# First FFN: eight up pairs as seven block products, and the weight sums of the last parts made by VectorE in the down products

## The chip, the core and the metric

The kernel runs on one core of a Trainium2 chip. A core has a matrix engine (TensorE, PE in the profile), a vector engine (VectorE, DVE), a scalar engine (ScalarE, ACT), GpSimd (POOL) and SyncE (SP); each works through its own list of instructions in order, and waits at an instruction until the semaphores that it names have come. The metric is the time of one execution in microseconds, the median of 3 runs.

## The reference

Two layers, each a mixer and then an FFN; the change lies in the FFN. With 528 positions (512 and 16 meta tokens), model width 1024 and FFN width 2816:

```python
def ffn_sublayer(h, pre_g, post_g, w_up, conv_w, w_down):
    u = rms_norm(h, pre_g)
    z = jnp.einsum("bld,df->blf", u, w_up)
    z = causal_depthwise_conv(z, conv_w)
    g, up = jnp.split(z, 2, axis=-1)
    y = jnp.einsum("blf,fd->bld", jax.nn.silu(g) * up, w_down)
    return h + rms_norm(y, post_g)
```

`w_up` is 1024 x 5632 and `w_down` 2816 x 1024 in each layer.

## The kernel before

**Matrix products.** All is float32. A matrix is split into a high and a low half that TensorE multiplies at full rate, and a product is three passes: high by high, high by low, low by high. `mm3` (L786) issues them for a list of blocks of 128 input channels. ScalarE makes the high half of a weight chunk by a cast (L601, `whi<-raw`), VectorE the low half by a subtraction (L602, `wlo<-raw,whi`). `prep_one` does this for one chunk of 512 KB: a load on SP's queue into one of three `raw` tiles, the cast, the subtraction. `next_w` calls it so that three chunks are ahead of the one that TensorE multiplies.

**The FFN of one layer.** The 2816 channels are 22 pairs: pair f has a gate chunk (f) and an up chunk (22 + f), of 128 channels each. They come in three parts, PARTS = (8, 7, 7). Within a part, each pair makes its two up products of 96 matmuls in all (8 blocks x 3 passes x 2 halves of 264 positions, twice), is copied from PSUM to `zs`, convolved (`gate_conv`: ACT L2120, then DVE L2122 twice), passed through silu (ACT L2132), multiplied (DVE L2133) and split into y (ACT L2136, DVE L2140). After a part, its down product runs in eight steps m, one for each 128 output channels; `yp` takes the result (ACT L2351 after part 0, DVE L2353 after part 1). The third part's down product is fused with the end of the layer.

**Seven block products.** For a pair listed in SEVEN, `seven_pair` takes the gate and up product together as a 2 x 2 block product (two halves of the input channels, two halves of the positions) and makes it with seven block products in place of eight: `product` (L2234) issues one, 4 blocks x 3 passes = 12 matmuls over half of the positions, so that a pair takes 84 matmuls in place of 96. It needs four weights: the first is half the plain gate and half plain; the three others (called c, b and d here, tags `whi`, `shi` and `y`) hold sums of blocks of the gate and up weights and come from a DRAM tile `w_sum`. It also needs sums of blocks of the input, `t0` to `t3`, which `normalised` builds while part 0 and its down product run. The results stand in PSUM and are combined by ScalarE's copies (L2260 to L2280).

Before, only layer 1 works so (SEVEN_IN), with 12 of its 22 pairs: 8 to 13 in part 1, 15 to 20 in part 2. The other tiles of a seven pair's weights are loaded into `h`: after part 0 of such a layer, h is written to DRAM, its space (four tiles of 512 KB, `spare`) serves as further raw tiles for four of every seven loads, and h is loaded back when the last seven pair is issued.

**The weight sums.** All 12 are made by DMA alone. `sum_steps` returns four steps: three copies into `w_sum` on SP's queue, and three accumulating DMAs on GpSimd's queue, one behind the other (L533). `tick` spreads them: a tiny copy on GpSimd (L2152) that reads what is just finished holds the queue until then. Eight pairs' sums are made in layer 0's FFN, four in layer 1's mixer.

**Split weights for the next mixer.** `store_one` takes six chunks of layer 1's `w_in`, splits them ahead of time (ACT L615, DVE L616) and stores both halves (`w_split`) on GpSimd's queue. It is called in layer 0's two down products, at the odd steps m.

**What sets the order.** In the FFN, a scheduler places each instruction by modelled times; what is written first goes first where times agree. Each engine's list is fixed when the program is built. A tile that is used again makes its next writer wait for its last reader.

## Time and profile before

| | |
|---|---|
| runs (3) | median 1282.54 us, 1281.57 to 1283.13 |
| the profiled execution | 1280.6 us, of which the span of the records is 1278.7 us |
| granted TensorE clock | 0.999 |
| layer 0's FFN | up part 0 from about 276 us, its down product from about 353 us, part 1 from about 400 us |
| layer 1's FFN | up part 0 to about 994 us, its down product to 1040.57 us |
| TensorE, up and down products of layer 0 | `mm3` L786 |
| seven block products (layer 1) | `product` L2234 |

The time includes about 2 us around the span. Busy time of an engine is the union of its instructions; the waits of TensorE, which has the least idle time, say where another engine or a transfer holds the kernel.

### The profile page before, as it was taken

The numbers are of one execution on the slowest core, as the hardware profiler recorded it, in microseconds if no ns is written. First come the engines' busy times: TensorE is split into PE (matmuls) and PEld (weight loads), VectorE is DVE, ScalarE is ACT, GpSimd is POOL, SyncE is SP. The second block draws the span as 40 slices with busy tenths as digits, with TensorE's granted clock in tenths as the row PEclk, the third lists the DMA queues.
The fourth block names the chain that finished last, engine by engine and source line by source line (L and its number), as shares of the span: only waits on it lengthen the run. The fifth ranks groups of instructions, "written<-read, shape, count | busy, mean of one in ns | idle before, by whom it ended". The sixth has DMA issues, their size and how long they took to land.

```text
span 1278.7 us, 24208 instructions
## 1 busy us (share of the span) xinstructions
PE 1259.6 (99%) x9660; PEld 1208.0 (94%) x9660; DVE 888.4 (69%) x1505; ACT 667.0 (52%) x1273; POOL 154.7 (12%) x333
## 2 busy tenths in 40 slices
PE   8999999999999999999999999999999999999997
PEld 8999899999999999999999998989999789979997
DVE  7888765688733774466587878765799738746964
ACT  7254577564333442233573546766554447626753
POOL 1313311001122112100003234120000000000000
PEclk9999999999999999999999999999999999999999
DMA  7136132705579647832461675536234235434611
GB/s 242 34 102 160 51 101 76 234 25 149 138 235 264 158 106 229 215 92 89 145 248 50 168 174 129 140 80 220 85 97 152 94 118 166 151 116 151 203 63 66
DMA packets 69393, 176.30 MB, mean 138 GB/s; under 512 B 7632, under 2 KB 18000, under 8 KB 69024
## 3 DMA queue, kind: packets, MB, share of 16 engines
q1 hardware_dynamic: 60784, 155.74, 38.4%
q0 software_dynamic: 8496, 19.01, 8.5%
q8 instruction: 76, 1.25, 0.4%
q14 instruction: 37, 0.30, 0.1%
HBM read 151.09 MB, written 37.95 MB: 148 GB/s over the span
## 4 chain that ended last, share of the span: by engine, by line
PE 93%; DVE 3%; ACT 1%; DMA 1%; issue 1%; POOL 0%; SPq 0%; DVEq 0%; ACTq 0%
PE psum L786 69%; PE psum L2234 9%; PE psum L1356 4%; PE psum L1620 3%; PE psum L1586 2%; PE psum L923 1%; PE psum L1542 1%; PE psum L1686 1%; PE psum L1272 1%; DMA raw<-in_w_dram 0%; DVE yp L999 0%; POOL dm L1557 0%; DMA h<-in_x_dram 0%; ACT whi L738 0%; DVE h L1009 0%
## 5 line engine op out<-in xcount | busy, mean ns | idle before, releaser
L786 PE MATMUL psum<-y,whi 128*128 128x264 f32 (+3 forms) x1968 | 384.1, 299 | 3.2 <-ACT yp L2351 1.7
L786 PE MATMUL psum<-uhi,whi 128*128 128x264 f32 (+1 forms) x1456 | 349.8, 288 | 2.7 <-DVE zs L2085 0.9
L786 PE MATMUL psum<-ulo,whi 128*128 128x264 f32 (+1 forms) x1456 | 343.4, 284 | 0.6 <-DVE ulo L2020 0.4
L786 PE MATMUL psum<-uhi,wlo 128*128 128x264 f32 (+1 forms) x1456 | 342.4, 284 | 0.0
L786 PEld LDWEIGHTS psum<-y,whi 128*128 128x128 f32 x1968 | 304.7, 188 | 17.5 <-ACT yp L2351 2.3
L786 PE MATMUL psum<-y,wlo 128*128 128x264 f32 (+3 forms) x984 | 272.7, 297 | 0.3 <-DVE wlo L742 0.3
L786 PEld LDWEIGHTS psum<-uhi,whi 128*128 128x128 f32 x1456 | 245.9, 188 | 7.4 <-issue 2.0
L786 PEld LDWEIGHTS psum<-ulo,whi 128*128 128x128 f32 x1456 | 246.0, 188 | 1.3 <-DVE ulo L2020 0.6
L786 PEld LDWEIGHTS psum<-uhi,wlo 128*128 128x128 f32 x1456 | 245.6, 188 | 0.0
L786 PEld LDWEIGHTS psum<-y,wlo 128*128 128x128 f32 x984 | 177.1, 188 | 5.7 <-DVE wlo L742 0.6
L601 ACT CAST whi<-raw 128x1024 fp32r<-128x1024 f32 (+1 forms) x80 | 82.2, 1029 | 114.4 <-PE psum L786 85.0
L2122 DVE SCALAR_TENSOR_TENSOR c<-zs,pv,c 128x528 f32<-128x528 f32 (+1 forms) x176 | 131.2, 757 | 11.2 <-ACT c L2120 9.2
L602 DVE TENSOR_TENSOR wlo<-raw,whi 128x1024 fp32r<-128x1024 f32 (+1 forms) x80 | 95.8, 1198 | 43.5 <-ACT whi L601 42.7
L742 DVE TENSOR_TENSOR wlo<-raw,whi 128x1024 fp32r<-128x1024 f32 (+2 forms) x80 | 95.6, 1204 | 29.8 <-ACT whi L738 29.3
L738 ACT CAST whi<-raw 128x1024 fp32r<-128x1024 f32 (+2 forms) x80 | 81.7, 1030 | 26.9 <-PE psum L786 20.0
L1102 DVE SCALAR_TENSOR_TENSOR cacc<-apad,pv,cacc 128x528 f32<-128x528 f32 x120 | 87.6, 772 | 0.1
L2120 ACT ACTIVATE c<-zs,pv 128x528 f32<-128x528 f32 (+1 forms) x88 | 63.2, 727 | 4.1 <-DVE zs L2272 1.5
L2136 ACT CAST y<-c 128x528 fp32r<-128x528 f32 (+1 forms) x44 | 27.6, 627 | 71.2 <-DVE c L2133 71.2
L2085 DVE TENSOR_TENSOR zs<-psum,rz 128x528 f32<-128x528 f32 x40 | 28.3, 707 | 47.7 <-PE psum L786 46.9
L1620 PE MATMUL psum<-pf,vals 128*128 128x400 f32 (+3 forms) x160 | 50.7, 399 | 0.6 <-POOL pf L1600 0.6
L1586 PE MATMUL psum<-q,k 128*128 128x128 f32 (+2 forms) x192 | 51.1, 348 | 0.0
L2132 ACT ACTIVATE c<-c 128x528 f32<-128x528 f32 (+1 forms) x44 | 28.1, 640 | 43.8 <-DVE c L2122 43.8
(265 smaller groups left out, 1972.5 us busy)
## 6 DMA issues: line engine op xcount, KB each, us to landing
raw<-in_w_dram SPq DMA_DIRECT2D x135, 512.0 KB, 4.3
raw<-in_w_dram SPq DMA_DIRECT2D x27, 448.0 KB, 4.4
h<-w_sum SPq DMA_DIRECT2D x14, 512.0 KB, 4.2
h<-in_w_dram SPq DMA_DIRECT2D x13, 512.0 KB, 3.8
w_sum<-in_w_dram SPq DMA_DIRECT2D x24, 256.0 KB, 8.5
w_sum<-in_w_dram SPq DMA_DIRECT2D x12, 512.0 KB, 7.3
w_sum<-in_w_dram POOLq DMA_DIRECT2D x12, 512.0 KB, 7.3
w_sum<-w_sum POOLq DMA_DIRECT2D x24, 256.0 KB, 5.6
```

Of the source, the lines that this page charges most:

```text
L601: nc.scalar.copy(hi[:, :sz], raw[:, :sz])
L602: nc.vector.tensor_sub(lo[:, :sz], raw[:, :sz], hi[:, :sz].bitcast(F32))
L738: nc.scalar.copy(box["hi"][:, :sz], box["raw"][:, :sz])
L742: nc.vector.tensor_sub(lo[:, :sz], box["raw"][:, :sz], box["hi"][:, :sz].bitcast(F32))
L786: nc.tensor.matmul(d, lhsT=w[a][:, k, cols], rhs=rhs(b, k, hf), start=start and i == 0 and p == 0, stop=stop and i == n - 1 and p == 2)
L1102: nc.vector.scalar_tensor_tensor(conv[j], in0=src, in1=conv[j], scalar=col("a_dw_w", CK * j + i), op0=ALU.mult, op1=ALU.add)
L1356: nc.tensor.matmul(ps[:n, :nw], lhsT=(uhi, ulo)[ui][:, k, P * b:P * b + n], rhs=w[wi][:, k % 4, :], start=k == 0 and p == 0, stop=k == KD ...
L1586: nc.tensor.matmul(s, lhsT=k[:, ka:ka + kn], rhs=q[:, s0:qz], start=i == 0, stop=i == 1)
L1620: nc.tensor.matmul(acc[:, s0 - qa:qz - qa], lhsT=vals[:, b].rearrange("p h d -> p (h d)")[:, o:o + P], rhs=box["p"], start=b == 0, stop=b ...
L2120: nc.scalar.activation(dst, src[:, 2:2 + 2 * fw], AF.Copy, scale=wtap(2, t))
L2122: nc.vector.scalar_tensor_tensor(dst, in0=src[:, i:i + 2 * fw], scalar=wtap(i, t), in1=dst, op0=ALU.mult, op1=ALU.add)
L2234: nc.tensor.matmul(psum[:, bank, :n7], lhsT=w[a][:, k0 + k, :], rhs=rhs(b, k), start=start and k == 0 and p == 0, stop=stop and k == K2 - ...
```

## The change

Layer 0 gets seven block products for eight pairs (12, 13, 15 to 20); layer 1 keeps its twelve. Twenty pairs therefore need sums, by two ways. Eight are made by DMA as before: layer 0's pairs 12 and 13 (in layer 0's own part 0), and layer 1's 8, 9, 10 (in layer 0's FFN) and 11, 12, 13 (in layer 1's mixer). The sums of the last six pairs of each layer are made by `down_sum`: GpSimd's queue loads the gate and up chunk into two of the four spare tiles in h, VectorE adds them in four additions of 128 x 512, and GpSimd's queue stores the results. Pairs 15, 16, 17 are done in part 0's down product and 18, 19, 20 in part 1's; for the j-th of them, the load stands at step 2j - 1, the additions at 2j + 1, the stores at 2j + 2. The third pair uses the tiles of the first again. While such tiles are in use (`in_spare`), no raw tile is taken from h.

`store_one` moves: it is called at m = 3, 5, 7 of part 0's down product and ahead of each of the pairs 8 to 11, takes its raw tile by `raw_tile` (so also from h), and splits into two single tiles of its own (`shi`, `slo`) rather than into those of the weight stream. `tick` no longer stands in the down products.

```diff
-SEVEN = (8, 9, 10, 11, 12, 13, 15, 16, 17, 18, 19, 20)
-SEVEN_IN = (1,)
-SUMS = {1: (8, 4)}
-SUM_US, SUM_LAT, SUM_EVERY = 0.9, 5.0, 40.0
+SEVEN = ((12, 13, 15, 16, 17, 18, 19, 20), (8, 9, 10, 11, 12, 13, 15, 16, 17, 18, 19, 20))
+SUMS = {0: (0, 0, 2), 1: (3, 3, 0)}
+DOWN_SUMS = 3
+SUM_US, SUM_LAT, SUM_EVERY = 0.9, 9.0, 40.0
...
+    def spare_tile(j):
+
+        return spare[0][:, 2 * j:2 * j + 2, :].rearrange("p a b -> p (a b)")
+
     def raw_tile():
 
-        if spare[0] is not None:
+        if spare[0] is not None and not in_spare[0]:
             n_raw[0] += 1
             j = (None, 0, None, 1, None, 2, 3)[n_raw[0] % 7]
             if j is not None:
-                return spare[0][:, 2 * j:2 * j + 2, :].rearrange("p a b -> p (a b)")
+                return spare_tile(j)
         return T(wp, [P, CHUNK], F32, "raw", 3)
+
+    def down_sum(l, f, q):
+
+        gate, up = (flat_w(up_chunk[l, t]) for t in (f, NF + f))
+        a, b = (spare_tile(2 * q + i)[:, :2 * SB] for i in range(2))
+        x, y = slice(0, SB), slice(SB, 2 * SB)
+
+        def load():
+            in_spare[0] += 1
+            nc.gpsimd.dma_start(a, gate)
+            nc.gpsimd.dma_start(b, up)
+
+        def add():
+            nc.vector.tensor_add(b[:, y], b[:, x], b[:, y])
+            nc.vector.tensor_add(b[:, x], a[:, x], b[:, x])
+            nc.vector.tensor_add(a[:, x], a[:, x], b[:, y])
+            nc.vector.tensor_add(a[:, y], a[:, x], a[:, y])
+
+        def store():
+            t = sums[l, f] = T(dram, [P, 4, SB], F32, f"w_sum{l}_{f}")
+            for i, src in enumerate((b, a)):
+                nc.gpsimd.dma_start(t[:, 2 * i:2 * i + 2], src.rearrange("p (e s) -> p e s", e=2))
+            in_spare[0] -= 1
+
+        return load, add, store
+
+    def down_sums(l, part):
+
+        fs = SEVEN[l][-2 * DOWN_SUMS:][DOWN_SUMS * part:DOWN_SUMS * (part + 1)]
+        at = {}
+        for j, f in enumerate(fs):
+            load, add, store = down_sum(l, f, j % 2)
+            for m, op in ((2 * j - 1, load), (2 * j + 1, add), (2 * j + 2, store)):
+                at.setdefault(m, []).append(op)
+        return at
...
-            hi, lo = (T(wx[0], [P, WCHUNK], F32R, t) if sz <= WCHUNK else T(wp, [P, CHUNK], F32R, t) for t in ("whi", "wlo"))
+            hi, lo = (T(tx[0], [P, 2 * SB], F32R, t) for t in ("shi", "slo")) if sz <= 2 * SB else (T(wp, [P, CHUNK], F32R, t) for t in ("whi", "wlo"))
...
-            raw = T(wp, [P, CHUNK], F32, "raw", 3)
+            raw = raw_tile()
...
+                    if l == 0 and part == 1 and f < seven[0]:
+                        store_one()
                     if f in seven:
                         seven_pair(f)
...
                 if part < len(PARTS) - 1:
+                    more = down_sums(l, part)
+                    for op in more.pop(-1):
+                        op()
...
+                            for op in more.pop(m, ()):
+                                with tc.issue_after(evac.ins), tc.issue_after(last_low[0].ins):
+                                    op()
-                            if l == 0 and m % 2:
+                            if l == 0 and part == 0 and m in (3, 5, 7):
                                 store_one()
-                            tick(yp[:, m, t0:t0 + 1])
```

Three places show what the new lists of the engines look like. The first is ScalarE at the end of layer 0's part 0 down product and the start of part 1, as it was: `yp` are the copies of the down steps, c_492 belongs to gate 8, whi_480 is the cast of gate 8's weights, whi_487 that of up 8's and whi_490 that of gate 9's.

```order
L601 CAST whi_480_4740<-raw_479_4738 128x1024
L2351 COPY yp_331_2812<-psum_1_67 128x528
L601 CAST whi_487_4808<-raw_486_4806 128x1024
L2351 COPY yp_331_2812<-psum_1_67 128x528
L601 CAST whi_490_4863<-raw_489_4861 128x1024
L2120 ACTIVATE c_492_4916<-zs_332_2813,pv0_3_69 128x528
L2132 ACTIVATE c_492_4916<-c_492_4916 128x528
L601 CAST whi_496_4935<-raw_495_4933 128x1024
```

And the same place of the changed kernel (its line numbers are some 46 higher; L2365 copies gate 8's result from PSUM, L661 is `store_one`'s cast, whi_484 are gate 8's weights, whi_487 up 8's, whi_497 gate 9's).

```order
L647 CAST whi_484_4745<-raw_483_4743 128x1024
L2402 COPY yp_331_2812<-psum_1_67 128x528
L661 CAST shi_493_4866<-raw_492_4862 128x1024
L2402 COPY yp_331_2812<-psum_1_67 128x528 x2
L2365 COPY zs_332_2813<-psum_1_67 128x264 x2
L2166 ACTIVATE c_501_4985<-zs_332_2813,pv0_3_69 128x528
L2178 ACTIVATE c_501_4985<-c_501_4985 128x528
L661 CAST shi_504_5002<-h_333_2820 128x1024
L647 CAST whi_487_4802<-h_333_2820 128x1024
L647 CAST whi_497_4876<-raw_496_4874 128x1024
```

The cast of up 8's weights stood ahead of the last copy of the down product, and now stands behind gate 8's copies, its convolution, its silu and a cast of `store_one`; it reads a tile of h rather than a raw tile. That tile's load waits on SP for the landing of pair 17's last store, which read the same tile.

The second is TensorE where gate 8 ends in the changed kernel. Its weights are whi_484 and wlo_485; whi_487 and wlo_488 are up 8's, whi_497 gate 9's.

```order
L832 MATMUL psum_1_67<-uhi_13_108,whi_484_4745 128x264 x2
L832 MATMUL psum_1_67<-ulo_14_109,whi_484_4745 128x264 x2
L832 MATMUL psum_1_67<-uhi_13_108,wlo_485_4746 128x264 x2
L832 MATMUL psum_1_67<-uhi_13_108,whi_487_4802 128x264 x2
L832 MATMUL psum_1_67<-ulo_14_109,whi_487_4802 128x264 x2
L832 MATMUL psum_1_67<-uhi_13_108,whi_497_4876 128x264 x2
L832 MATMUL psum_1_67<-ulo_14_109,whi_497_4876 128x264 x2
L832 MATMUL psum_1_67<-uhi_13_108,wlo_488_4803 128x264 x2
L832 MATMUL psum_1_67<-uhi_13_108,whi_487_4802 128x264 x2
```

Up 8's first matmuls still follow gate 8's last ones at once, and four matmuls of gate 9 now stand between up 8's fourth and fifth; before, gate 9's began after up 8's last.

The third is TensorE at pair 15 of layer 0, after part 1's down product, as it is now: whi_592 is the pair's first weight (the rows ahead of these are its second block product), whi_595 and wlo_596 are its c, shi_598 its b, and whi_602 is pair 16's first weight.

```order
L2280 MATMUL psum_1_67<-uhi_13_108,whi_592_6109 128x264
L2280 MATMUL psum_1_67<-ulo_14_109,whi_592_6109 128x264
L2280 MATMUL psum_1_67<-uhi_13_108,wlo_593_6110 128x264
L2280 MATMUL psum_1_67<-t0_401_3689,whi_595_6160 128x264 x2
L2280 MATMUL psum_1_67<-uhi_13_108,whi_602_6247 128x264
L2280 MATMUL psum_1_67<-ulo_14_109,whi_602_6247 128x264
L2280 MATMUL psum_1_67<-t2_403_3691,shi_598_6211 128x264 x2
L2280 MATMUL psum_1_67<-t2_403_3691,slo_599_6212 128x264
```

In the code the product with c is second; in the built order three products of the pair (the first with whi_592, the first with shi_598, the second with whi_592) go ahead of it, and eleven matmuls of other products come between its second and its third. Before, this place held `mm3`'s plain up products with whi_579 and wlo_580, without any product of sums.

More of the change, by code (lines that the diff above doesn't have):

```diff
@@ L533, in put, with last @@
             nc.gpsimd.dma_start(to, src, accum_op=ALU.add)
+        def last():
+            put(t[:, 3], t[:, 2])
+            sums[l, f] = t
+        moves = [(t[:, 0], up[:, :SB]), (t[:, 1], up[:, :SB]), (t[:, 2:4], gate.rearrange("p (e s) -> p e s", e=2))]
         def copies():
             with tc.issue_after(last_load[0].ins):
-                nc.sync.dma_start(t[:, 0], up[:, :SB])
-                nc.sync.dma_start(t[:, 1], up[:, :SB])
-                nc.sync.dma_start(t[:, 2:4], gate.rearrange("p (e s) -> p e s", e=2))
-        return copies, lambda: put(t[:, 0:2], diag), lambda: put(t[:, 2], t[:, 1]), lambda: put(t[:, 3], t[:, 2])
+                for to, src in moves:
+                    nc.sync.dma_start(to, src)
+        return copies, lambda: put(t[:, 0:2], diag), lambda: put(t[:, 2], t[:, 1]), last
     def sums_at(l, place):
@@ L546, in sums_at @@
         n0 = sum(counts[:place])
-        return SEVEN[n0:n0 + counts[place]] if place < len(counts) else ()
+        return SEVEN[l][n0:n0 + counts[place]] if place < len(counts) else ()
     pw_place = [None]
@@ L2145, in tile_hybrid_trunk @@
             late_ups = deque()
-            seven = SEVEN if l in SEVEN_IN else ()
-            todo = deque(step for to, place in ((l + 1, 0), (l, 2)) for f in sums_at(to, place) for step in sum_steps(to, f))
+            seven = SEVEN[l]
+            todo = deque(step for to, place in ((l, 2), (l + 1, 0)) for f in sums_at(to, place) for step in sum_steps(to, f))
             def tick(src):
```

15 lines of the change are left out of this document (8 added, 7 removed).

## Prediction

> **What bounds the kernel now.** I read the page first: the busy time of each engine, and the chain that ended last.
>
> ```profile
> span 1278.7 us, 24208 instructions
> PE 1259.6 (99%) x9660; PEld 1208.0 (94%) x9660; DVE 888.4 (69%) x1505; ACT 667.0 (52%) x1273; POOL 154.7 (12%) x333
> PE 93%; DVE 3%; ACT 1%; DMA 1%; issue 1%; POOL 0%; SPq 0%; DVEq 0%; ACTq 0%
> ```
>
> TensorE is busy for 99% of the span, and 93% of the chain is its work. So a matmul that goes is worth its duration, and every wait of TensorE that comes is a loss in full: nothing else is late enough to absorb it. Then the chain of layer 0's FFN (start, length, what):
>
> ```profile
> 276.68 87.86 PE psum L786 x720
> ...
> 364.58 0.60 ACT yp L2351
> ...
> 365.23 58.63 PE psum L786 x480
> ...
> 423.91 0.71 DVE zs L2085
> ...
> 424.76 69.01 PE psum L786 x560
> ...
> 493.87 0.72 DVE yp L2353
> ...
> 494.63 122.39 PE psum L786 x1002
> ```
>
> Four long runs of matmuls with three short waits between them. One matmul of 264 positions is worth 87.86 / 720 = 0.122 us; a plain up product is 48 of them, 5.86 us. The part 0 down product starts two steps before the wait at 364.58, at about 352.8 (eight steps of 48 matmuls, 46.9 us, and 0.6 for the wait), so part 1 starts at about 400.3 and gate 8 ends at about 406.2. Last, what layer 1 does with seven block products now:
>
> ```profile
> 1040.00:1108.00 68.00, 68.00 (x565) 67.75 (x564) 52.02 (x69) 47.63 (x85) 0.00 (x0) 1.00 0.51 164
> 1040.57 49.24 PE psum L2234 x408
> ```
>
> In this row of the stretches (length; busy PE, PEld, DVE, ACT, POOL; clock; DMA share; GB/s) TensorE is busy for 68.00 of 68.00 us, with VectorE at 52.02 and ScalarE at 47.63. The form itself therefore costs no waits once its weights are ready, and saves what it says.
>
> **The change part by part.** *The matmuls.* Eight pairs go from 96 to 84 matmuls of 264 positions: 8 x 12 x 0.122 = 11.7 us. Two more are added to prime PSUM: 0.24. Net **-11.5 us**, all on TensorE and so on the path.
>
> *The old waits.* The wait at 423.91 was for VectorE's scaling of an up product out of PSUM, which ScalarE's copies replace here. I take -0.6; bounds 0 and -2.0 (all three waits).
>
> *The additions.* Each is a VectorE operation of 128 x 512; the nearest row:
>
> ```profile
> L2133 DVE TENSOR_TENSOR c<-c,c 128x512 f32<-128x512 f32 x22 | 15.2, 689 | 0.6
> 494.60:618.00 123.40, 123.31 (x1009) 123.08 (x1010) 74.53 (x90) 43.40 (x54) 12.74 (x20) 1.00 0.53 149
> 365.00:425.00 60.00, 58.85 (x482) 58.68 (x483) 22.20 (x23) 19.84 (x26) 14.44 (x23) 1.00 0.86 241
> ```
>
> Four take 2.8 us a pair, three pairs a down product, 8.3 us beside 47 us of matmuls. VectorE had 22.20 us of work in the 60 us around layer 0's first down product (third row): there is room, so I cost them at nothing by themselves. Without that cover they would cost up to 2.8 a step. The input sums that layer 0 must now build stand in the same place as in layer 1, where they wait for nobody. What decides is the time at which the transfers around the additions let a tile go.
>
> *Up 8 in layer 0* (the first two order pieces). The cast of up 8's weights now stands on ScalarE behind gate 8's copies from PSUM, and those can start only when gate 8's last matmul ends. TensorE's next matmul needs that cast. The steps between the two, by the rows of the same operations:
>
> ```profile
> L2270 ACT COPY zs<-psum 128x258 f32<-128x258 f32 x12 | 4.5, 371 | 0.0
> L2120 ACT ACTIVATE c<-zs,pv 128x528 f32<-128x528 f32 x44 | 32.0, 734 | 1.3 <-DVE zs L2085 1.3
> L2122 DVE SCALAR_TENSOR_TENSOR c<-zs,pv,c 128x528 f32<-128x528 f32 x88 | 66.8, 766 | 1.4
> L2132 ACT ACTIVATE c<-c 128x528 f32<-128x528 f32 x22 | 14.2, 646 | 40.1 <-DVE c L2122 40.1
> L601 ACT CAST whi<-h 128x1024 fp32r<-128x1024 f32 x13 | 13.7, 1050 | 15.0 <-PE psum L786 12.8 <-issue 1.9
> ```
>
> Two copies 0.74, the convolution 0.73 on ScalarE and 2 x 0.77 on VectorE, silu 0.65, `store_one`'s cast 1.05, up 8's cast 1.05: 5.75 us, and some six hand-overs of about 0.05 (the "issue" pieces of 0.04 in the chain), so 6.0. The four matmuls of gate 9 that stand behind up 8's fourth need one more cast, 1.05, of which up 8's four cover 0.49: 0.6 more. **+6.6 us**, of which nothing can be hidden, since all of it stands in order between two matmuls. It can be more if the tile isn't there yet. Up 8's cast would start at 406.2 + 4.9 = 411, 58 us after the down product's start; its tile waits for the landing of pair 17's last store. The transfers:
>
> ```profile
> w_split<-whi POOLq DMA_DIRECT2D x6, 512.0 KB, 4.9
> w_split<-wlo POOLq DMA_DIRECT2D x6, 512.0 KB, 7.8
> h<-w_sum SPq DMA_DIRECT2D x14, 512.0 KB, 4.2
> h<-in_w_dram SPq DMA_DIRECT2D x13, 512.0 KB, 3.8
> L619 POOL DMA_DIRECT2D w_split<-whi x6: 552/575/605, 356.7 to 504.0; - x6
> ```
>
> A 512 KB transfer of GpSimd's queue is seen to land in 4.9 to 7.8 us (L), and to take 0.58 us of GpSimd's time. Pair 15's additions end after two steps (12.3) and 2.8; its store, pair 17's load into the same tile, 2.8 of additions, the store, and SP's load for up 8 follow each other, with about six issues (3.5): 21.4 + 4 L at most, which is 41 to 52.6 us. GpSimd's queue also carries the `w_split` stores, each issued in order behind a wait, up to one more L: 60.4. So 0 to 2.4 more; I take 0, since most of the range fits. Range 6.6 to 9.0.
>
> *Pair 15 in layer 0* (the third piece). The product with b now runs right behind the first, and ScalarE must copy the first's result between them: 0.37 and two hand-overs, 0.5, without cover. Then c, whose tile waits for pair 20's store. The additions end at 0.7 + 6 x 5.12 + 2.8 = 34.2 us after the down product's start (a step is 42 matmuls), then issue, landing, load 4.2 and cast 1.05: 44.9 to 47.8, and the matmuls get there at 0.7 + 41.0 + 3 x 1.46 + 0.5 = 46.6. With the 0.5: 0.5 to 1.7, and up to 3 if the queue is a further issue or two late. I take **+1.5**.
>
> *Layer 1.* The order of TensorE stays, but b of pair 8 now waits for pair 17's store: 21.4 + 4 L again, 41 to 52.6, against about 48.6 (from the chain of waits: the down product starts at about 993.7, its last piece ends at 1040.57, two block products of 1.45 follow, less the cast). 0 to 4; by the middle, L = 6.4, it fits by 1.6. Pair 15 there is the same as in layer 0. I take **+1** for both, range 0 to 5.
>
> *The rest.* `store_one` uses single tiles around pairs 8 to 11, so that each call waits for the last one's stores: cast 1.05, subtraction 1.2, issue 0.6, landing 4.9 to 7.8 make 7.8 to 10.7 us against 11.7 for a pair. It fits. The mixer of layer 1 makes three sums rather than four; a chunk cast stands ahead of a copy in the first down steps. +0.5 for all, between -1 and +2.5.
>
> Sum: -11.5 - 0.6 + 6.6 + 1.5 + 1 + 0.5 = **-2.5 us**. It is made against the profiled execution, 1280.6 us (span 1278.7), which lies 1.9 below the median of the runs. Against that median: 1282.5 - 2.5 = **1280.0**.
>
> **The rivals.** *The order costs, and the clock falls too (1282.7).* A wait of 6 us of TensorE occurs nowhere in the trace; its longest are these, and only the start of the program shows it after rest:
>
> ```profile
> PE psum L1030 <- DVE yp L999: 1.4, 1, 1.4
> L1983 PE MATMUL psum<-warm 128*128 128x264 f32 x44 | 8.1, 365 | 1.3 <-DVE warm L1981 1.3
> ```
>
> Behind rest, 44 matmuls of 264 positions took 8.1 us, where 44 x 0.122 = 5.4: a loss of 2.7 us. If a wait of 6 us is rest enough, the same 2.7 comes on top. For it: the cold start is plain. Against it: no row shows a restart in between, and the wait is broken by four matmuls. 1280.0 + 2.7 = 1282.7.
>
> The Trainium skill ("TensorE: Matmul & The Clock Gate", Part 1: The HAM clock gate) states that TensorE falls to half its clock after an idle window of about 3.4 us, and takes about as long at work to come back. By that rule this rival would hold; no run here shows it yet beyond the cold start.
>
> *The transfers set the end (1288, slower).* If GpSimd's transfers land in 7.8 us or more beside the weight stream (the row of 365 to 425 has DMA busy for 0.86 of the time), the chain with its four landings decides at three places: up 8 +2.4, pair 15 +1.5 more, pair 8 of layer 1 and its pair 15 +4. Together 7.9: 1288. It decides from L = 6.8 in layer 1 ((48.6 - 21.4) / 4). For it: 7.8 is the median of the low halves' stores. Against it: the accumulating DMAs and their copies leave that stretch. The Trainium skill ("DMA: Bandwidth & Descriptors", Anatomy of one DMA) gives a fit of 2.0 us plus size over 436 KB/us for GpSimd's queue, 3.2 us for 512 KB; by it none of these would be late, but the rows here are longer.
>
> *Only up 8's order costs (1277).* If all transfers are in time and the casts at pair 15 fit, the terms of 1.5, 1 and 0.5 shrink to 0.5, 0 and -0.5: -5.5. For it: layer 1's 68.00 of 68.00 today.
>
> **How the numbers follow.** Forecast 0.40, clock 0.22, transfers 0.18, only up 8's order 0.20. The forecast's own range is 1277 to 1284. With the rivals, 8 in 10 lie between 1275.5 and 1288.5. About 0.2% (2.6 us) is what a measurement can tell from no change: below 1280.0 faster, above 1285.1 slower. Forecast half below; only up 8's order nearly always; the clock 0.15, so faster 0.42. The transfers nearly always slower, the clock a quarter, the forecast 0.05: slower 0.25. Same 0.33.
>
> **What would show it.** Right: 94 matmuls fewer; TensorE waiting 6 us at up 8 for ScalarE's cast, behind copies, convolution and silu; waits of up to 2 us at layer 0's pair 15. Matmuls of about 0.24 us behind up 8's wait would show the clock. If the wait there ends with a transfer into h, or pair 8 of layer 1 waits for one, it is the transfers. It would be wrong if that cast is on time, or if the longer wait is one that I priced at nothing: the additions ahead of the down product's copies, or `store_one`'s single tiles.

## The result, and the profile after

| | before | changed |
|---|---|---|
| runs on one chip | 4: median 1282.05 us, 1281.38 to 1283.13 | 4: median 1293.73 us, 1290.61 to 1296.96 |
| ratio | | **1.0091**, 95% interval 1.0064 to 1.0117 |
| the profiled execution | 1280.6 us, span 1278.7 | 1290.61 us, span 1288.9 |
| granted clock | 0.999 | 0.994 |

The changed kernel is slower, by some 12 us. It does 94 matmuls fewer, as it should, and its span is 10.2 us longer all the same (1288.9 against 1278.7). First the page of the changed kernel: span, busy time of each engine, and the shares of the chain that ended last.

```profile
span 1288.9 us, 24302 instructions
PE 1253.6 (97%) x9566; PEld 1200.7 (93%) x9566; DVE 935.1 (73%) x1593; ACT 708.4 (55%) x1373; POOL 164.6 (13%) x357
PE 81%; DMA 7%; DVE 5%; issue 3%; ACT 2%; POOL 1%; SPq 0%; DVEq 0%; ACTq 0%; POOLq 0%
```

TensorE is busy for 6.0 us less than before (1259.6), but its share fell from 99% to 97%, and DMA, which had 1% of the chain, now has 7%. So new waits came, and transfers end them. The waits of TensorE (line waited for, and then us in total, times, longest):

```profile
PE psum L832 <- ACT whi L647: 8.8, 1, 8.8
PE psum L2280 <- ACT whi L647: 4.8, 2, 4.4
PE psum L832 <- ACT yp L2402: 1.9, 3, 1.0
PE psum L2280 <- ACT whi L637: 1.6, 1, 1.6
```

The third row is copies behind down products; the others are casts of weights, and new. The 8.8 is up 8 of layer 0, the 4.4 is pair 8 of layer 1, the 1.6 is pair 15 of layer 0. Next, stretches of the changed kernel around these places (length; busy PE, PEld, DVE, ACT, POOL with counts; granted clock; DMA share; GB/s). The first two rows are the end of gate 8 and the wait, the third and fourth what follows it, then the same behind pair 15's waits and behind layer 1's.

```profile
400.30:406.70 6.40, 5.97 (x49) 5.83 (x48) 1.22 (x1) 1.03 (x3) 1.06 (x2) 1.00 1.04 381
406.70:415.80 9.10, 0.29 (x3) 0.08 (x1) 2.73 (x3) 4.14 (x7) 0.53 (x1) 0.80 0.72 268
415.84:419.10 3.26, 3.26 (x15) 3.25 (x16) 3.26 (x3) 2.83 (x3) 0.53 (x1) 0.52 0.92 256
419.10:424.00 4.90, 4.90 (x43) 4.90 (x42) 1.44 (x2) 0.40 (x2) 0.80 (x2) 1.00 1.00 378
542.00:545.00 3.00, 3.00 (x16) 3.00 (x15) 1.01 (x1) 0.46 (x2) 0.00 (x0) 0.50 0.96 266
1049.60:1053.40 3.80, 3.80 (x19) 3.61 (x20) 1.97 (x3) 1.58 (x4) 0.00 (x0) 0.61 0.48 142
```

A wait costs twice. In the third row 15 matmuls take 3.26 us, 0.22 us each at a clock of 0.52; 15 x 0.122 would be 1.8, so 1.4 us are lost behind the wait. The fifth row loses 3.00 - 16 x 0.122 = 1.0, the sixth 3.80 - 19 x 0.122 = 1.5. By the fourth row the clock is back. The Trainium skill ("TensorE: Matmul & The Clock Gate", Part 1: The HAM clock gate) states half the clock after an idle window of about 3.4 us, and about as long to return; rows three and six agree. Row five does not: it stands behind waits of 0.5 to 1.6 us only (the last section comes back to it).

**Up 8.** The chain of the changed kernel into that wait (start, length, what):

```profile
386.54 4.38 DMA h<-in_w_dram
...
391.01 0.70 DVE h L595
...
393.45 10.30 DMA w_sum<-h
...
403.81 10.92 DMA h<-in_w_dram
...
414.75 1.05 ACT whi L647
...
415.84 7.80 PE psum L832 x50
```

Read from the end: TensorE starts at 415.84, behind the cast, which starts when SP's load of up 8's weights into h has landed (414.73). That load was issued at 403.81, when the last sum's store, which read the same tile, had landed: 10.30 us after its issue. That store stood behind the additions, and these behind GpSimd's load of 386.54. Why that load is so late shows in the same kernel's GpSimd list (start, length, instruction, idle time before it and what ended it):

```profile
368.62 0.59 POOL L602 DMA_DIRECT2D w_sum<-h  x1 [8.80 <-DVE h L595]
...
374.81 0.53 POOL L591 DMA_DIRECT2D h<-in_w_dram  x1 [3.50 <-DMA w_sum<-h]
375.85 0.53 POOL L602 DMA_DIRECT2D w_sum<-h  x1
...
386.54 0.54 POOL L590 DMA_DIRECT2D h<-in_w_dram  x1 [7.28 <-DMA w_sum<-h]
```

The third pair uses the first pair's two tiles again. The first store leaves at 368.62, the second at 375.85; its landing lets the load go at 386.54, 10.7 us later. GpSimd's own order holds it too: the second sum was ready at 373.69, but GpSimd stood at the load of 374.81, ahead of that store in its list, until the first store had landed. Last, ScalarE in that wait:

```profile
406.91 0.66 ACT L2365 COPY zs<-psum 128x264 f32<-128x264 f32 x2 [5.58 <-PE psum L832]
409.98 0.64 ACT L2178 ACTIVATE c<-c 128x528 f32<-128x528 f32 x1 [1.64 <-DVE c L2168]
413.53 1.04 ACT L661 CAST shi<-h 128x1024 fp32r<-128x1024 f32 x1 [2.91 <-DMA h<-in_w_dram]
414.75 1.04 ACT L647 CAST whi<-h 128x1024 fp32r<-128x1024 f32 x1 [0.17 <-DMA h<-in_w_dram]
```

Gate 8's copies, convolution and silu do stand ahead of the two casts, but ScalarE is done with them at 410.62. Then it idles 2.91 us until a transfer into h brings `store_one`'s chunk, and 0.17 for up 8's. So of the 9.0 us (start to start of matmuls, less one matmul), about 3.1 is late transfers, and 5.9 is the order of the lists in this build.

**Layer 1** has the same chain at pair 8, with its wait of 4.55 us:

```profile
1027.32 5.80 DMA h<-in_w_dram
...
1035.65 6.46 DMA w_sum<-h
1042.12 5.30 DMA h<-w_sum
...
1048.48 1.05 ACT whi L647
1049.57 49.88 PE psum L2280 x398
```

And VectorE in the changed kernel just ahead of it (1028.99 is the first of the third pair's four additions):

```profile
1028.99 0.69 DVE L594 TENSOR_TENSOR h<-h 128x512 f32<-128x512 f32 x1
1033.21 0.69 DVE L595 TENSOR_TENSOR h<-h 128x512 f32<-128x512 f32 x1 [3.53 <-DMA h<-in_w_dram]
...
1035.27 1.22 DVE L648 TENSOR_TENSOR wlo<-raw,whi 128x1024 fp32r<-128x1024 f32 x1
```

The second addition needs the late load, and VectorE, which works in order, stands for 3.53 us. The low half of the weight stream's next chunk (L648) is behind it. Layer 0 has the same, 3.75 us at 391.01. This could be a second path to the same place, since a late low half frees its raw tile late. In this trace it held SP for 0.3 us only; the load that TensorE waited for (1042.12) stood behind the last sum's store. GpSimd's order counts here as in layer 0: pair 16's first sum was ready at 1021.86, but its store stood behind the load of 1027.32 in GpSimd's list and left at 1027.84. SP waited 10.1 us, until 1034.37, for that store to land.

### The profile page after: what moved, and what is told of

It reads as the page before. It is cut to its first block, busy times and chain, and to the rows that moved or that the text cites. A ratio compares the mean times of both kernels' runs of the same rounds, so it can differ in the third digit from the quotient of the medians.

```text
span 1288.9 us, 24302 instructions
## 1 busy us (share of the span) xinstructions
PE 1253.6 (97%) x9566; PEld 1200.7 (93%) x9566; DVE 935.1 (73%) x1593; ACT 708.4 (55%) x1373; POOL 164.6 (13%) x357
## 4 chain that ended last, share of the span: by engine, by line
PE 81%; DMA 7%; DVE 5%; issue 3%; ACT 2%; POOL 1%; SPq 0%; DVEq 0%; ACTq 0%; POOLq 0%
PE psum L832 52%; PE psum L2280 15%; PE psum L1402 4%; PE psum L1666 3%; DMA h<-in_w_dram 2%; DMA w_sum<-h 2%; PE psum L1632 2%; PE psum L969 1%; PE psum L1588 1%; DMA h<-w_sum 1%; DVE c L2168 1%; PE psum L1732 1%; DVE wlo L648 1%; PE psum L1318 1%; ACT whi L647 1%
## 5 line engine op out<-in xcount | busy, mean ns | idle before, releaser
L832 PE MATMUL psum<-uhi,whi 128*128 128x264 f32 (+1 forms) x1200 | 298.5, 289 | 10.9 <-ACT whi L647 8.8
L832 PE MATMUL psum<-ulo,whi 128*128 128x264 f32 (+1 forms) x1200 | 292.4, 284 | 0.6 <-DVE ulo L2066 0.4
L832 PE MATMUL psum<-uhi,wlo 128*128 128x264 f32 (+1 forms) x1200 | 290.9, 284 | 0.0
L832 PEld LDWEIGHTS psum<-uhi,whi 128*128 128x128 f32 x1200 | 206.7, 189 | 15.9 <-ACT whi L647 9.1
L832 PEld LDWEIGHTS psum<-uhi,wlo 128*128 128x128 f32 x1200 | 206.2, 189 | 0.0
L648 DVE TENSOR_TENSOR wlo<-raw,whi 128x1024 fp32r<-128x1024 f32 (+1 forms) x70 | 83.0, 1186 | 17.8 <-ACT whi L647 17.6
L2280 PE MATMUL psum<-uhi,whi 128*128 128x258 f32 (+1 forms) x240 | 68.3, 285 | 4.8 <-ACT whi L647 4.8
L2280 PE MATMUL psum<-ulo,whi 128*128 128x258 f32 (+1 forms) x240 | 67.7, 283 | 0.0
L2280 PE MATMUL psum<-uhi,wlo 128*128 128x258 f32 (+1 forms) x240 | 67.5, 283 | 0.0
L2280 PE MATMUL psum<-t,shi 128*128 128x258 f32 (+1 forms) x320 | 61.2, 287 | 0.9 <-ACT psum L2306 0.5
L2280 PEld LDWEIGHTS psum<-t,shi 128*128 128x128 f32 x320 | 50.3, 192 | 1.3 <-ACT psum L2306 0.7
```

Of the source, the lines that this page charges most:

```text
L648: last_low[0] = nc.vector.tensor_sub(lo[:, :sz], raw[:, :sz], hi[:, :sz].bitcast(F32))
L832: nc.tensor.matmul(d, lhsT=w[a][:, k, cols], rhs=rhs(b, k, hf), start=start and i == 0 and p == 0, stop=stop and i == n - 1 and p == 2)
L2280: nc.tensor.matmul(psum[:, bank, :n7], lhsT=w[a][:, k0 + k, :], rhs=rhs(b, k), start=start and k == 0 and p == 0, stop=stop and k == K2 - ...
```

## The experiments

Two theories were on the table for the new waits. **Tiles**: the loads that follow the last sum go into the tiles that its store has just read. **Additions**: VectorE stands at the third pair's additions, and the weight stream behind it. Rivals for the sizes were the order on ScalarE (up 8), `store_one`, the DMA traffic itself, and the seven block form. Times of one run have no interval; the kernel before lay at 1280.1 to 1280.7 us (medians) on these chips.

**No sums at all (e2_nosums).** What the form itself is worth. The products with c and b take plain gate and up weights, and no sums are made, by DMA or VectorE; this leaves the sums of the weights out.

```diff
...
-                t = sums[seven_up[i]]
-                parts.extend((("c", t[:, 1::2]), ("b", t[:, 0:3:2]), ("d", flat_w(i)[:, SB:])))
+                l7, f7 = seven_up[i]
+                c7, b7 = (flat_w(up_chunk[l7, t]).rearrange("p (e s) -> p e s", e=2) for t in (f7, NF + f7))
+                parts.extend((("c", c7), ("b", b7), ("d", flat_w(i)[:, SB:])))
...
```

> The changed kernel with no weight sums at all: the block products load the plain gate and up weights where the sums stood, so the output is not the reference's. It shows what the block products in layer 0 are worth alone. If the form costs nothing by itself: 12 us less than the kernel before, about 1270. If building the input sums, ScalarE's copies or the extra loads cost time by themselves: 1275 or more.

Measured: 1266.71 us (4 runs), ratio 0.989 [0.9873, 0.9906]; span 1264.8, 13.9 below before. No wait of TensorE over 1.4 us is left in the profile. So the matmuls are worth what was said, the order of TensorE costs nothing, and all of 1288.9 - 1264.8 = 24.1 us comes with the sums.

**Another place for the next loads (e1_ring5).** The five raw loads behind each part's last store take raw tiles, none of h.

```diff
+        if hold[0] and not in_spare[0]:
+            hold[0] -= 1
-        if spare[0] is not None and not in_spare[0]:
+        elif spare[0] is not None and not in_spare[0]:
...
             in_spare[0] -= 1
+            hold[0] = 5
```

> The changed kernel, but the five weight loads behind each part's last sum take the ring of raw tiles and none of h. Theory (a load that waits for the last store of the sums holds a cast, and TensorE with it): the wait of 9.0 us at up 8, most of the 2.9 us at layer 0's pair 15 and the 4.6 us at layer 1's pair 8 go, and the slow matmuls behind them (about 1.5 us each) with them: some 18 to 20 us less than the changed kernel, 1272 to 1276. Rival (the added transfers fill the DMA engines, whatever tile they go to): the waits stay in size but end with a load into a raw tile; 1288 or more.

Measured: 1281.83 us (10 runs), ratio 1.0015 [1.0005, 1.0024]. Up 8's wait is gone whole, with the same matmuls and the same `store_one`: so neither piece of the 9.0 us followed from the change's order alone: with other tiles for the loads, both go. But the waits of TensorE in this kernel show two others (its lines are 3 higher):

```profile
PE psum L2283 <- ACT zs L2368: 4.9, 1, 4.9
PE psum L2283 <- ACT whi L650: 4.4, 1, 4.4
```

The first is new, at pair 12 of layer 0; the second is layer 1's pair 8, as large as before. Fewer tiles for the stream move the shortage on. Whether layer 1's wait is one of the tiles this run cannot say: there SP still stood 10.1 us, until 1025.32, at a load into h for the landing of a sum's store, and the load of pair 8's b stood behind it. So the edit did not free layer 1 of the tiles.

**Matmuls in the wait (e3_filler).** Is the slow stretch behind up 8's wait the clock, or a late operand? 66 matmuls whose result nobody reads are put behind gate 8.

```diff
...
+                        if l == 0 and i == 2 * PARTS[0]:
+                            gate_end = last_mm[0]
+                            for _ in range(66):
+                                with tc.issue_after(gate_end.ins):
+                                    nc.tensor.matmul(psum[:, 0, :H], lhsT=ones_r, rhs=uhi[:, 0, :H], start=True, stop=True)
```

> The changed kernel with 66 matmuls of 264 positions that nobody reads between gate 8 and up 8 (8.0 us at full clock, in a wait of 9.0). Theory (TensorE's clock falls behind a wait of this length): the first matmuls of up 8 take 0.12 us rather than 0.22, and up 8 ends 1.5 us earlier than without. Rival (they are slow because their weights or their inputs come slowly): they stay at 0.22 us.

Measured: 1287.26 us (one run). Stretches of this kernel, behind the filled wait and behind pair 15 of layer 0:

```profile
415.20:418.50 3.30, 3.10 (x23) 2.88 (x24) 3.30 (x4) 2.71 (x3) 0.53 (x1) 1.00 0.76 237
539.40:545.00 5.60, 5.46 (x23) 5.15 (x24) 3.42 (x3) 2.34 (x4) 0.00 (x0) 0.50 0.62 188
```

Behind the filled wait the clock stays at 1.00: there it falls because TensorE rests. At pair 15, where this kernel happened to idle 3.84 us, 23 matmuls take 5.46 us at 0.50; in layer 1 its wait was only 1.5 us, and no slow matmul followed.

**Layer 1's sums alone (e4_sums1).** The kernel before, with only layer 1's last six sums made by VectorE; layer 0 stays plain, `store_one` and `tick` as they were.

```diff
-SEVEN = ((12, 13, 15, 16, 17, 18, 19, 20), (8, 9, 10, 11, 12, 13, 15, 16, 17, 18, 19, 20))
-SUMS = {0: (0, 0, 2), 1: (3, 3, 0)}
+SEVEN = ((), (8, 9, 10, 11, 12, 13, 15, 16, 17, 18, 19, 20))
+SUMS = {1: (6, 0)}
...
```

> The kernel before, with only the last six weight sums of layer 1 made by VectorE in its down products, and the other six by DMA; layer 0 has plain products and store_one where it was. Theory (the sums alone make layer 1's wait): a wait of about 4.5 us at pair 8 and 1.7 us of slow matmuls behind it, 1286 to 1289. Rival (it is the work that layer 0's change pushes into layer 1): no new wait, 1281 to 1283.

Measured: 1302.52 us (one run); in layer 1 waits of 5.4 us at pair 8, 4.4 at pair 15 and 1.3 + 1.85 in the last down product, slow matmuls behind the large ones. So layer 1's loss needs nothing of layer 0's part of the change. It is larger here than in the changed kernel; why was not settled (other tiles fall to the loads, by their count).

**Two sums a part (e5_two).** No third pair, so no tile is used twice; the sums left over go to the mixer, and layer 0 has six such pairs.

```diff
-SEVEN = ((12, 13, 15, 16, 17, 18, 19, 20), (8, 9, 10, 11, 12, 13, 15, 16, 17, 18, 19, 20))
-SUMS = {0: (0, 0, 2), 1: (3, 3, 0)}
-DOWN_SUMS = 3
+SEVEN = ((12, 13, 17, 18, 19, 20), (8, 9, 10, 11, 12, 13, 15, 16, 17, 18, 19, 20))
+SUMS = {0: (0, 0, 2), 1: (3, 5, 0)}
+DOWN_SUMS = 2
```

> The changed kernel with two sums per down product rather than three (17, 18 and 19, 20 of each layer), so that no spare tile is used twice and the last store stands at m = 4; layer 0 has six pairs of seven block products (12, 13, 17 to 20), layer 1 its twelve, of which eight are summed by DMA. Theory (the chain load, add, store, load, add, store through two tiles ends too late for the next part's first weights): no wait over 1 us at up 8, at pair 15 or at layer 1's pair 8, full clock, 6 x 12 x 0.122 = 8.8 us less than the kernel before, 1271 to 1274. Rival (any sums made beside the down product's weights hold the stream): waits of 3 us or more at the parts' ends stay, 1280 or more.

Measured: 1287.86 us (4 runs), ratio 1.0064 [1.0043, 1.0085]. Up 8's, pair 15's and layer 1's waits are gone, as the third pair is; small new ones stand in layer 0 (1.6 us in the down product, 2.1 at pair 12). The gain is lost in the mixer, which is 11.1 us longer than before: its five sums now hold GpSimd (the longest wait of TensorE in this kernel):

```profile
PE psum L1666 <- POOL pf L1646: 7.5, 3, 7.0
```

**Without `store_one` (e6_nostore)**, which takes raw tiles from h and shares GpSimd's queue.

```diff
-MASK = "111111000000000000000000"
+MASK = "000000000000000000000000"
```

> The changed kernel without store_one: the six chunks of the next mixer are loaded and split in the mixer like the others. Theory (the landings of 9 to 11 us at up 8 come from transfers that stand close together, six of them store_one's): the sums' stores in layer 0 land in 5 to 7 us, up 8 waits for less than 4 us, layer 1 waits as before (4 to 5 us at pair 8); the mixer loses some us by itself. Rival (the sums' own chain is late by itself): up 8 waits 7 us or more.

Measured: 1286.59 us (one run). Up 8's wait is gone, pair 15 of layer 0 keeps 1.5 us, layer 1 still has 3.8 at pair 8, and 4.2 at pair 15, which is new. The mixer pays some 5 us for weights that are not split ahead. So `store_one` has a part in up 8's wait, and layer 1's does not need it.

**Without the additions (e7_noadds).** The loads and stores of the six pairs stay, the four additions are left out, so that the stored sums hold plain weights.

```diff
-            nc.vector.tensor_add(b[:, y], b[:, x], b[:, y])
-            nc.vector.tensor_add(b[:, x], a[:, x], b[:, x])
-            nc.vector.tensor_add(a[:, x], a[:, x], b[:, y])
-            nc.vector.tensor_add(a[:, y], a[:, x], a[:, y])
```

> The changed kernel without VectorE's additions: gate and up chunks are loaded and stored as they are, so the sums hold plain weights and the output is not the reference's. All transfers stay. Theory (the transfers decide): the waits at up 8 and at layer 1's pair 8 fall by no more than 2 to 3 us each, the additions' own time in the chain; 1286 or more. Rival (the chain is late because the additions queue behind VectorE's other work, as the first of them end 26 us after the down product's start): the waits vanish, 1270 or less.

Measured: 1274.8 us (one run). Layer 1's waits vanish, up 8's too; 2.4 and 2.8 us are left in layer 0. But the stores move as well, since they no longer wait for a sum. GpSimd's last store of layer 1's first down product in this kernel:

```profile
984.56 0.54 POOL L599 DMA_DIRECT2D w_sum<-h  x1 [4.60 <-DMA h<-in_w_dram]
```

It leaves some 3.8 us before TensorE starts that down product; in the changed kernel it leaves at 1035.65, 38.3 us after the start. So the same transfers cost layer 1 nothing when they come early. The run does not part VectorE's wait from the late stores.

**Placing with care (e8_smart).** The eight loads behind the last store alternate between raw tiles and tiles 2 and 3 of h, which the middle pair let go earlier.

```diff
             j = (None, 0, None, 1, None, 2, 3)[n_raw[0] % 7]
+            if late[0]:
+                late[0] -= 1
+                j = (2, None, 3, None)[late[0] % 4]
...
             in_spare[0] -= 1
+            late[0] = 8
```

> The changed kernel, where the eight loads behind each part's last sum take turns between the ring and the two spare tiles that pair 16 or 19 used (stored two steps earlier), and leave out the two tiles of the last sum. Theory (what holds is a weight load that waits for the last store in its tile, and a ring too short without spare tiles): no wait at up 8 and at layer 1's pair 8 and pair 15; transfers in layer 0 remain close together, a wait of up to 5 us about pair 12; 1272 to 1280. Rival (transfers too many, any tile): layer 1 waits 3 us or more at pair 8 as with the ring alone; 1282 or more.

Measured: 1279.64 us (7 runs), ratio 0.9985 [0.9969, 1.0002]. Up 8's wait is gone; 3.2 us at pair 12, 0.8 + 0.9 at pair 15, and layer 1 keeps 5.15 us. In layer 1 of this kernel, SP's wait (line, what for; us in total, times, longest), and GpSimd's list just ahead of its end:

```profile
SPq L633 <- DMA w_sum<-h: 9.9, 1, 9.9
```

```profile
1015.18 0.53 POOL L593 DMA_DIRECT2D h<-in_w_dram  x1 [6.46 <-DMA w_sum<-h]
1015.70 1.06 POOL L605 DMA_DIRECT2D w_sum<-h  x2
```

So a store of a sum still holds the weight stream. The sum was ready at 1010.0, but GpSimd stood 6.46 us at the load ahead of it in its list; the store left at 1015.70, and SP waited for its landing until 1022.27 before it could load b. ScalarE's list adds to it. The cast of pair 8's first weight, whose chunk had landed at 1010.02, stands behind the cast of b, at which ScalarE waited 12.68 us, so TensorE gets that weight only after 1030.08.

**`store_one` elsewhere (e9_move, e10_both).** It is called in part 0 of layer 0, at pairs 2 to 7 and at m = 1; e10_both is this and e8_smart.

```diff
-                    if l == 0 and part == 1 and f < seven[0]:
+                    if l == 0 and part == 0 and f >= 2:
...
-                            if l == 0 and part == 0 and m in (3, 5, 7):
+                            if l == 0 and part == 0 and m == 1:
```

> The changed kernel with store_one in layer 0's part 0 (at pairs 2 to 7 and at m = 1 of its down product) rather than in the down product and part 1. Theory (in layer 0 it is store_one's loads, cast and stores that made up 8 and pair 15 late): up 8 waits for less than 2 us, as without store_one, and the mixer keeps the prepared chunks; layer 1 waits as in the changed kernel; 1278 to 1284. Rival (its work in part 0 comes late there): new waits in part 0, 1287 or more.

> Both edits together: store_one in part 0 of layer 0, and the eight loads behind the last sum only in the ring and in pair 16's or 19's tiles. Theory: no wait over 2 us in either FFN, full clock, 1267 to 1273, below both kernels. Rival (VectorE's additions come late whatever the tiles): 3 us or more stay at layer 1's pair 8; 1276 or more.

Measured: e9_move 1287.3 us (one run), e10_both 1282.36 (10 runs), ratio 1.001 [0.9995, 1.0025]. Both have new waits of about 3.3 and 2.0 us in part 0 and its down product, and keep layer 1's (4.7 and 4.0). Moving these stores only moves the shortage.

**Later additions (e11_late).** The third pair's additions stand two steps later, its stores follow at once at m = 7; nothing else.

```diff
-            for m, op in ((2 * j - 1, load), (2 * j + 1, add), (2 * j + 2, store)):
+            d = 2 * (j == 2)
+            for m, op in ((2 * j - 1, load), (2 * j + 1 + d, add), (min(2 * j + 2 + d, 7), store)):
```

> The changed kernel, with only one edit: the additions of each part's third pair stand two steps later (m = 7 rather than 5), so that VectorE finds their chunks landed and the low halves of the weight stream go ahead of them; the stores follow at once. Theory (VectorE waits in order at an addition for its load, 3.5 us, and the stream's subtractions stand behind it): layer 1's wait at pair 8 falls below 2 us, although the last store comes later. Rival (the reused tile alone decides): the wait grows to 6 us or more, since its store comes later.

Measured: 1295.38 us (one run). VectorE no longer waits; its groups of the second addition, in the changed kernel and in this one (count, busy us, mean ns, idle us before):

```profile
L595 DVE TENSOR_TENSOR h<-h 128x512 f32<-128x512 f32 x12 | 8.2, 686 | 7.3 <-DMA h<-in_w_dram 7.3
```

```profile
L595 DVE TENSOR_TENSOR h<-h 128x512 f32<-128x512 f32 x12 | 8.2, 684 | 0.1
```

The 7.3 us are the 3.75 and the 3.53 seen above. Yet layer 1 waits 5.4 us at pair 8, now for c, whose load leaves late:

```profile
1043.85 6.05 DMA h<-w_sum
...
1050.95 1.05 ACT whi L648
...
1052.05 8.04 PE psum L2281 x52
```

The stores come later now, and the loads still go into their tiles (SP stood 6.2 us for a sum's store here). From layer 1's part 1 on this kernel loses 19.8 us beside the kernel without sums, where the changed kernel loses 6.9; the rest of that was not traced. Layer 0 loses 8.9 rather than 17.0. Either edit alone (e8, e11) leaves a wait of some 5 us in layer 1.

**Both (e12_late_smart).** The edits of e8 and e11 together.

> The later additions, and the eight loads behind the last sum in the ring and in pair 16's or 19's tiles only. Theory: no wait over 1.5 us in layer 1's FFN; in layer 0 the wait at pair 12 stays (3 to 5 us and slow matmuls behind it), from store_one's and the copies' transfers; 1270 to 1276. Rival (landings at random, wherever the loads go): layer 1 waits 3 us or more somewhere; 1278 or more.

Measured: **1267.95 us** (4 runs, 1266.74 to 1269.4), ratio **0.9904** [0.9889, 0.9918]: 12.3 us below the kernel before, and faster than both kernels. Its page (span, busy time), and its stretches of part 1 in the two layers:

```profile
span 1265.0 us, 24315 instructions
PE 1247.0 (99%) x9566; PEld 1195.6 (95%) x9566; DVE 935.1 (74%) x1593; ACT 708.0 (56%) x1373; POOL 164.0 (13%) x357
```

```profile
400.40:479.50 79.10, 79.10 (x651) 79.10 (x649) 54.91 (x67) 46.68 (x79) 15.48 (x24) 1.00 0.82 267
1021.00:1098.90 77.90, 77.90 (x626) 76.61 (x625) 59.65 (x80) 51.67 (x92) 3.18 (x6) 1.00 0.60 204
```

The same two stages of the changed kernel:

```profile
400.90:491.40 90.50, 81.08 (x649) 80.65 (x649) 54.08 (x65) 47.70 (x80) 14.14 (x22) 0.96 0.78 234
1038.00:1122.00 84.00, 79.60 (x625) 78.12 (x624) 57.27 (x76) 51.68 (x92) 2.12 (x4) 0.98 0.58 188
```

TensorE is busy throughout, at full clock, with the same additions (DVE 935.1 us in both kernels). The two stages are 11.4 and 6.1 us shorter, and the span, 1265.0, is that of the kernel without sums. What became of up 8's order shows on ScalarE in this kernel:

```profile
400.34 1.05 ACT L652 CAST whi<-raw 128x1024 fp32r<-128x1024 f32 x1
401.30 0.59 ACT L2407 COPY yp<-psum 128x528 f32<-128x528 f32 x1
...
409.42 0.65 ACT L2370 COPY zs<-psum 128x264 f32<-128x264 f32 x2
```

Up 8's cast stands ahead of the last copy of the down product again, as in the kernel before, reads a raw tile, and is done 8 us before gate 8's copies. In layer 1, SP still waits 9.6 us (until 1016.87) for the landing of a sum's store. But b now goes into a raw tile, and the cast of the pair's first weight (1015.41) stands ahead of b's (1022.22) on ScalarE; in e8 it stood behind. The edits change these lists together, so the run shows that the placing removes the waits, and not which list does it. The wait at pair 12 of layer 0 went as well, which I had expected to stay, since `store_one` and its transfers are unchanged; by which link the later additions free it is open.

**Both, and `store_one` in part 1 (e13_late_smart_move)**, at pairs 9 to 11 and at m = 1, 3, 5, 7 of its down product.

```diff
-                    if l == 0 and part == 1 and f < seven[0]:
+                    if l == 0 and part == 1 and 8 < f < seven[0]:
...
-                            if l == 0 and part == 0 and m in (3, 5, 7):
+                            if l == 0 and part == 1 and m in (1, 3, 5, 7):
```

> As the one before, and store_one moved out of layer 0's first down product, to pairs 9 to 11 and to m = 1, 3, 5, 7 of part 1's down product. Theory: layer 0 waits for less than 3 us in all, no slow matmuls; 1267 to 1272, below both kernels. Rival (its transfers then make pair 15 late): a wait of 3 us or more there; 1274 or more.

Measured: 1277.98 us (10 runs), ratio 0.9977 [0.9963, 0.9991]; a wait of 4.8 us is back ahead of pair 12. The change's own places for `store_one` are the better ones.

Not all came as expected. e8 landed in its range and e12 some 2 us below its own; e1, e4, e5, e9, e10 and e13 came out longer than theirs. e7 lay between its theory and its rival, and e11 missed its theory, by which layer 1 was to wait less than 2 us.

## Why the prediction was wrong

- **The matmuls (-11.5) and the old waits (-0.6): right.** Without the sums the span falls by 13.9, 1.8 more than the two terms; where these lie was not traced.
- **"I cost them at nothing by themselves": the step that failed, and with it the sum "21.4 + 4 L".** I priced the additions by their busy time and by VectorE's room. As work they do cost nothing: e12 has all of them, at the time of the kernel without sums. What failed is when they end. Pair 15's additions were to end 15.1 us (12.3 + 2.8) after the down product's start. They ended 20.9 us after it in layer 0 (352.74 to 373.69) and 19.8 in layer 1 (997.40 to 1017.17), because VectorE has other work between the four: 365.90 to 373.69 is 7.8 us for 2.8 of additions. The third pair's second addition then waits 3.5 to 3.75 us more for its load. GpSimd's list was not in the sum either: a load that waits for a landing holds finished sums behind it, in layer 1 by some 6 us. In layer 1 the four landings took 6.89, 5.80, 6.46 and 5.30 us, within my L, so there the start and the lists were late, not the transfers.
- **What the experiments part, and what they do not.** With one of the two edits, 5.15 us (e8) or 5.4 (e11) stay at layer 1; with both, none. Each edit moves several lists at once. So the placing of the sums and of the loads behind them is shown as the cause, but the shares of VectorE's wait, of GpSimd's list, of ScalarE's order and of the tiles stay open.
- **Layer 1: +1 forecast, range 0 to 5; measured 6.2 in part 1** (84.0 against 77.8 before, by the starts of the same matmuls), of which 4.55 is the wait at pair 8 and about 1.5 the clock. Part 2 adds 0.7.
- **Up 8: +6.6 forecast, up to 9.0; measured 9.0, and 1.4 of clock behind it.** Place, cast and order were as forecast. The term was mis-sized because of "I take 0" for the transfers. SP's load for up 8 landed 62.0 us after the down product's start, where I had 41 to 52.6, and 60.4 at most. I held L to 4.9 to 7.8 us, medians over the whole kernel, and three of the four landings that count here took 10.7, 10.30 and 10.92 us, at DMA shares of 0.92, 1.03 and 0.88. Why they took so long was not tried: full engines alone do not say it, since a store of layer 1 landed in 6.46 us at a share of 1.02. And "nothing can be hidden, since all of it stands in order" did not hold beyond this build: with other tiles (e12) up 8's cast stands ahead of the copies, and up 8 costs nothing. The order on ScalarE came with the late tile; I took it for a cause of its own.
- **Pair 15 of layer 0: +1.5 forecast, up to 3; measured 2.9** in three waits (0.6, 1.7, 0.6), and slow matmuls behind them. Part 2 of layer 0 is 4.8 us longer than without sums (77.7 against 72.9).
- **The rest: +0.5 forecast.** A wait of 0.7 at pair 12 of layer 0, and 0.3 in the mixer and layer 1's first part beside the kernel without sums; about right.
- **The rivals.** I set the clock and the transfers against each other, and gave the clock one place. Both happened, and at three places: transfers that ended late made waits, and slow matmuls lengthened each by 1.0 to 1.5 us (3.9 in all). Added up, the rivals' own prices above the forecast (2.7 and 7.9) give 1290.6, most of the way to 1293.73; as exclusive cases they ended my range at 1288.5.
- **The sum.** Against the kernel without sums, by the starts of the same matmuls, the changed kernel loses 0.5 in layer 0's first down product, 11.4 in part 1, 4.8 in part 2, 0.3 up to layer 1's part 1, 6.2 and 0.7 in layer 1's parts 1 and 2: 23.9 of the 24.1 us. For the same places the forecast had 6.6 + 1.5 + 1 + 0.5 = 9.6.

## What to carry to other kernels

An instruction that waits at the head of an engine's list costs whatever stands behind it for as long as its data is late, not its busy time. Here that was VectorE's addition (3.5 us), GpSimd's load ahead of finished sums (6 us) and, in e8, ScalarE's cast of b (12.68 us). So ask of each instruction that you put into a list when its data lands, and what stands behind it. Where a chain of load, work and store ends in a buffer, let the next stage's first loads go to buffers that were let go earlier, and place the work only once its load has landed. Here the other buffers alone brought the kernel level with the one before (1279.6 us), the later work alone gained nothing (1295.4, one run), and both together came out 12 us below the kernel before. Two rivals with one cause (a late transfer, and the clock behind the wait that it makes) are one case, and their prices add.

## What the hardware showed that I had not expected

- TensorE's clock fell behind rests, and behind some short ones. The rests of 3.09 us and more (3.09 and 3.29 in e9 and e10, 3.84 in e3, 4.40 and 8.85 in the changed kernel) were each followed by matmuls at some 0.22 us in place of 0.122, at a granted clock of 0.50 to 0.61. Between 1.5 and 3.1 us the runs differ. In e7 a single rest of 2.26 us (at 420.7 us) was followed by 16 matmuls at a clock of 0.60, and one of 2.67 us by none; in e8 one of 3.06 us was followed by none. At pair 15 of layer 0 in the changed kernel no single idle time passed 1.6 us (0.5, 1.6 and 0.4 within 7 us), and 16 matmuls at 542 us still ran at a clock of 0.50. So these runs give no single threshold; these cases go against a rule of one idle window, and what triggers the fall was not tried.
- Transfers of 512 KB that land in a median of 4.5 us (GpSimd's loads) or 6.5 us (its stores of sums) over the kernel took 10.3 to 10.9 us at up 8, two stores and one of SP's loads, at DMA shares of 0.88 to 1.03 (297 to 415 GB/s). What made them so long is open. The Trainium skill ("DMA: Bandwidth & Descriptors", Anatomy of one DMA) gives a fit by which I estimate 3.2 us for 512 KB on GpSimd's queue; beside a weight stream the trace does not agree.

```profile
w_sum<-h POOLq DMA_DIRECT2D x24, 512.0 KB, 6.5
h<-in_w_dram POOLq DMA_DIRECT2D x24, 512.0 KB, 4.5
```

- Kernels with large waits spread more: 1290.61 to 1296.96 us in 4 runs of the changed kernel, against 1266.47 to 1267.01 in 4 of the kernel without sums. What differs from run to run was not traced.
